# The sample's matmul runs are placed behind the prompt's value products, and the gates are multiplied five blocks later

## The chip, the cores and the metric

The kernel runs on one core of one Trainium2 chip. A core has a matrix engine (TensorE, PE in the profile; its weight loads are shown apart as PEld), a vector engine (VectorE, DVE), a scalar engine (ScalarE, ACT), a general engine (GpSimd, POOL) and a queue engine (SyncE, SP) that issues most transfers here; 16 DMA engines move the data. Each engine works through its own list of instructions in order, and semaphores tie the lists together. The metric is the device time of one execution in microseconds.

## What is computed

One inference step of a small hybrid decoder, in float32, for two groups of tokens at once: a prompt of 2048 new tokens, and a sample of 8 sequences with 8 new tokens each, which look back on 4096 cached positions. One recurrent layer (RG-LRU) comes first, then keys, values and a forget term are made once from its output, then one attention layer uses them:

```python
def fox_block(q, k, v, cq, ck, q_pos, k_pos):
    s = jnp.einsum('bqhd,bkhd->bhqk', q, k).astype(jnp.float32) * (HEAD_DIM ** -0.5)
    s = s + jnp.swapaxes(cq, 1, 2)[:, :, :, None] - jnp.swapaxes(ck, 1, 2)[:, :, None, :]
    mask = k_pos[None, :] <= q_pos[:, None]
    s = jnp.where(mask[None, None], s, -jnp.inf)
    p = jax.nn.softmax(s, axis=-1)
    return jnp.einsum('bhqk,bkhd->bqhd', p.astype(v.dtype), v)
...
def fox_mixer(x, k, v, cq, ck, q_pos, k_pos, w_in, w_out):
    z = x @ w_in
    q = z[..., :D_ATTN].reshape(B, T, N_HEADS, HEAD_DIM)
    g = z[..., D_ATTN:]
    o = fox_attention(q, k, v, cq, ck, q_pos, k_pos).reshape(B, T, D_ATTN)
    return (o * jax.nn.silu(g)) @ w_out
```

There are 16 heads of width 64. The prompt attends to itself (`_p` outputs); the sample attends to `past_k = cache_k[page_table]`, 32 pages of 128 rows for each of the 8 sequences, and to its own new rows. All keys and values of the cache together are what the sample has to read: 8 x 32 pages of 512 KB each, twice.

## The kernel before

The program is written in Python, which traces instructions in an order of its own; a planner then orders each engine's list at build time, by a simulated clock: what is ready and of the highest priority (normally the earliest traced) goes first. `tc.add_manual_dep(..., ORDER)` and `tc.issue_after` force one instruction behind another on its engine, and `tc.high_priority()` lets a block go ahead of what is traced before it.

The stages are: the recurrent layer in two chunks; the shared projection of keys, values, queries and gates (`phase_b`), with the decode of the sample beside it; the prompt's attention (`attention`), with the rest of the decode beside it; and the output projection (`project`).

**The prompt's attention.** 64 units of (head, 512 queries) are worked in blocks of 128 keys; there are 640 blocks, and the loop at line 1585 counts them as `tick`. A block has two score matmuls `st` (lines 1592, 1593), on the diagonal a third (1595), the exponential on ACT (1601) into a tile `p`, and, some 18 blocks ahead, one matmul `sx` (1431) whose row maximum DVE takes (1433, 1435). After every fourth block, two blocks late, `product` emits the value products `ops` of those four blocks as one uninterrupted group (`together`, 1616) and POOL adds the `p` tiles up (1620). `later.after(n, fn)` is a list of callbacks that are due n blocks on. At the end of two heads (a pair) `total` sums on PE and sends the sums away, and five blocks after the pair's last unit `norm` (1492) takes reciprocals and sends them by two small DMAs into the tile `rr` (r in the trace). For each of the four query chunks `fetch` loads the stored gate `sg` (1521), and three blocks later `gate` (1503) has one matmul `rp` (1505) spread `rr` over the partitions and POOL and DVE multiply output and gate.

**The decode beside it.** A turn is one sequence and half of the heads (16 turns; 13 of them in `phase_b`'s second half and in the attention). It has eight loads of four pages of keys and eight of values, which share four buffers `raw`, as do two helper tiles (`spare`). Keys: DVE transposes a load in two parts (1180) into `ktr` tiles, of which there are two; after four loads `scores` emits a run of 32 small matmuls `dS` (1148) for each part, into the PSUM bank with the tag "d". Then comes the softmax (`softmax`). Values: `products` emits a run of eight small matmuls `dO` (1262) for each load, and these wait for its four DMAs. `period` interleaves the loads of three neighbouring turns; every step yields a cost (a key step QK 700, a value step two times 510, a softmax step HOP 300), and `Side.along` runs the decode in proportion to the cost of the attention's blocks. `t.dl` is a list of callbacks like `later` that counts the turn's own steps: value runs were emitted one step after their load was asked for, key runs one or two steps after the transposes. PE's position for a run comes from `behind("T", first)`: it stands behind the latest `st` matmul that had been traced (line 1592 sets `place["T"]`), and the other matmuls of the run follow it at high priority.

The transfers are issued by SP in order; a load of pages waits there until its `raw` buffer is free (1093).

Of the kernel before, what the change touches and what calls it, by code (L numbers as in the profile page):

```python
# [60 lines left out]
AFT = 14  # L61

# [25 lines left out]
def tile_hawk_fox(  # L88
# [27 lines left out]

    def paged():

        return tc.issue_after(place["S"]) if "S" in place else ExitStack()

    def together(mms, after=(), beside=False):

        first = mms[0]().ins
        for d in after:
            tc.add_manual_dep(first, d.ins.name, SYNC)
        if beside:
            behind("T", first)
        with tc.high_priority(), tc.issue_after(first):
            for mm in mms[1:]:
                mm()  # L130
# [912 lines left out]
    def decode(es, turns, nraw, nktr, ahead):  # L1043
# [31 lines left out]
        def spare():  # L1075
            if ahead:
                return pool.tile([P, 2048], F32, name="sy", tag="raw", bufs=nraw)
            return pool.tile([P, 4096], F32, name="sy", tag="ktr", bufs=nktr)[:, :2048]

        def pages(cache, b, hg, g):  # L1080

            with ExitStack() as order:

                if len(last) >= 3:
# [3 lines left out]
                    skip_runtime_bounds_check_because="the table was held between the first page and the last")[1]  # L1088
            raw = pool.tile([P, 4, 512], F32, name="raw", tag="raw", bufs=nraw)
# [40 lines left out]
        def keys(t, xs):  # L1130
# [40 lines left out]
            for x in xs:  # L1171
                g, n = divmod(x, 4)
                if n == 0:
                    t.kts = [pool.tile([P, 4, 4, 256], F32, name="ktr", tag="ktr", bufs=nktr) for _ in range(2)]
# [4 lines left out]
                for pp in range(2):  # L1179
                    behind("V", V.transpose(t.kts[pp][:, n], raw[:, :, pp * 256:(pp + 1) * 256]).ins)  # L1180
                    if n == 3:
                        dl.after(1 + pp, lambda g=g, pp=pp, kt=t.kts[pp]: scores(g, pp, kt))
# [5 lines left out]
        def softmax(t):  # L1188
# [5 lines left out]
            while dl.q:  # L1194
                dl.tick()
                yield HOP

# [52 lines left out]
        def values(t, xs):  # L1250
# [83 lines left out]
    def attention(es):  # L1334
# [157 lines left out]
        def norm(pr, sums, q0, n, oT):  # L1492
# [25 lines left out]
            def fetch(qc):  # L1518
# [64 lines left out]

        for u, (h, qc) in enumerate(units):
            for k in range(nks[u]):
# [17 lines left out]
                def product(u=u, h=h, todo=pair, acc=acc, last=(k == nks[u] - 1)):  # L1603
# [6 lines left out]
                    def mm(k, lo, p, r):  # L1610
# [5 lines left out]
                    together([partial(mm, k, lo, p, r) for k, lo, p, _ in todo for r in range(2) if lo <= (2 + r) * P],  # L1616
                             [todo[-1][3]])
# [11 lines left out]
                tick += 1  # L1629
                later.tick()  # L1630
# [230 lines left out]
    place.clear()  # L1861
    side.upto(1e12)
# [38 lines left out]
```

## Time and profile before

| | us |
|---|---|
| median of 3 runs | 3023.98 |
| lowest and highest | 3017.05, 3034.43 |
| the profiled execution | 3028.43 |
| its span, first to last instruction | 3026.4 |

| engine | busy us | share of the span |
|---|---|---|
| PE | 2803.4 | 93% |
| DVE | 1805.5 | 60% |
| ACT | 1269.9 | 42% |
| POOL | 1084.4 | 36% |

The attention's first score matmul starts at 1749 us, the decode's last value run at 2709 us, the attention's last product at 2871 us; after it only the output projection is left. In the profile's rows a group is one line, engine and operation with its tiles (output <- inputs) and shapes: 128*32 in front of a shape means that the matmul uses 32 columns of the 128 x 128 array, 128*64 that it uses 64, 128*128 all. A float32 matmul of the small kind leaves two records, so a value run of 8 matmuls shows as x16, a key run of 32 as x64, a product of four blocks as x16 (x14 on the diagonal). A matmul's printed time holds its way through the array and overlaps the next; the time that it takes from the engine is read from start to start. "PEclk" is the granted clock of PE as a share of the full one.

### The profile page before, as it was taken

What the parts mean: (1) busy time and instruction counts of PE and PEld (TensorE: products, weight loads), DVE (VectorE), ACT (ScalarE), POOL (GpSimd) and SP (SyncE); (2) the same over time, 40 slices, a digit from 0 to 9 for tenths busy, and PEclk for the clock granted to TensorE, in tenths of its full rate; (3) what the DMA queues carried; (4) which work ended last, traced back from release to release, by engine and by line L of the source; (5) the groups of instructions that cost most, each with busy time, mean ns of one, the idle gap of its engine ahead of it and who ended that gap; (6) DMA issues with size and microseconds to landing.
All of it is one profiled execution on the core that took longest, in us unless ns stands there. A gap on an engine that the chain in (4) does not pass through costs nothing.

```text
span 3026.4 us, 60467 instructions
## 1 busy us (share of the span) xinstructions
PE 2803.4 (93%) x21614; PEld 2252.1 (74%) x21614; DVE 1805.5 (60%) x4012; ACT 1269.9 (42%) x2874; POOL 1084.4 (36%) x1199
## 2 busy tenths in 40 slices
PE   6998999998997999999999699998998999999998
PEld 5997789988887997888889556665665666565687
DVE  6877455425427775676564466656776756655344
ACT  4665342222125665534333234444544444355321
POOL 1653201000002653100000245665575656659422
PEclk9999999999998999999999889999999999999999
DMA  4224546888863226699999968898899888874343
GB/s 123 79 88 133 171 126 191 256 263 281 278 216 91 89 88 194 209 313 338 332 346 326 279 209 243 248 282 255 250 291 287 267 251 265 260 247 122 98 145 110
DMA packets 479103, 653.79 MB, mean 216 GB/s; under 512 B 91291, under 2 KB 277020, under 8 KB 471525
## 3 DMA queue, kind: packets, MB, share of 16 engines
q1 hardware_dynamic: 475174, 644.26, 67.4%
q10 hardware_dynamic: 3340, 3.56, 0.4%
q8 instruction: 171, 2.80, 0.4%
q0 software_dynamic: 288, 2.10, 0.2%
q14 instruction: 130, 1.06, 0.1%
HBM read 514.22 MB, written 135.16 MB: 215 GB/s over the span
## 4 chain that ended last, share of the span: by engine, by line
PE 59%; DMA 16%; DVE 9%; ACT 6%; SPq 5%; issue 3%; POOL 1%; ACTq 0%; DVEq 0%; POOLq 0%
PE ops L1612 7%; PE st L1592 4%; PE y L383 4%; PE y L384 4%; PE y L385 4%; DMA raw<-in_cache_k_dram 4%; PE sx L1431 4%; PE dO L1262 3%; DMA raw<-in_cache_v_dram 3%; PE st L1593 3%; PE dS L1148 3%; PE kv L383 3%; PE kv L385 3%; PE kv L384 3%; SPq L1093 2%
## 5 line engine op out<-in xcount | busy, mean ns | idle before, releaser
L108 POOL TENSOR_TENSOR acc<-acc,p 128x512 f32<-128x512 f32 (+3 forms) x576 | 640.9, 1114 | 347.7 <-PE ops L1612 211.2
L1601 ACT ACTIVATE p<-st 128x512 f32<-128x512 f32 (+3 forms) x576 | 291.3, 525 | 400.1 <-PE st L1593 177.5
L1180 DVE STREAM_TRANSPOSE ktr<-raw 128x1024 f32<-128x1024 f32 x256 | 308.2, 1226 | 125.1 <-DMA raw<-in_cache_k_dram 116.5
L1433 DVE TENSOR_REDUCE mxs<-sx 128x1 f32<-128x512 f32 x384 | 255.0, 681 | 141.0 <-PE sx L1431 139.6
L383 PE MATMUL kv<-wh,xh 128*128 128x256 f32 (+3 forms) x1088 | 310.0, 288 | 6.4 <-ACT wh L427 4.7
L384 PE MATMUL kv<-wl,xh 128*128 128x256 f32 (+3 forms) x1088 | 309.3, 287 | 5.7 <-DVE wl L428 5.7
L385 PE MATMUL kv<-wh,xl 128*128 128x256 f32 (+3 forms) x1088 | 309.6, 286 | 2.7 <-DMA xl<-xld 2.7
L1592 PE MATMUL st<-qa,ka 128*128 128x512 f32 (+3 forms) x640 | 269.9, 422 | 13.3 <-ACT p L1601 7.5
L1612 PE MATMUL ops<-p,vvt 128*64 128x256 f32 (+1 forms) x2176 | 262.9, 369 | 1.0 <-ACT p L1601 0.7
L1431 PE MATMUL sx<-kbt,qbt 96*128 96x512 f32 (+3 forms) x640 | 229.2, 416 | 29.9 <-DMA qbt<-qd 24.2
L1113 POOL TENSOR_TENSOR qw<-qb,amask 128x128 f32<-128x128 f32 x64 | 29.1, 460 | 618.1 <-PE dS L1148 325.3
L428 DVE SCALAR_TENSOR_TENSOR wl<-wst,gv,wh 128x256 fp32r<-128x256 f32 (+1 forms) x384 | 169.4, 504 | 131.8 <-ACT wh L427 131.5
L427 ACT ACTIVATE wh<-wst,gv 128x256 fp32r<-128x256 f32 (+1 forms) x384 | 164.6, 499 | 190.2 <-DMA wst<-in_w_kv_dram 72.7
L1593 PE MATMUL st<-qbt,kbt 128*128 128x512 f32 (+3 forms) x640 | 236.9, 370 | 0.0
L383 PE MATMUL qg<-xh,wh 128*128 128x512 f32 (+2 forms) x640 | 229.4, 359 | 0.0
L384 PE MATMUL qg<-xl,wh 128*128 128x512 f32 (+2 forms) x640 | 228.2, 357 | 0.0
L385 PE MATMUL qg<-xh,wl 128*128 128x512 f32 (+2 forms) x640 | 227.5, 356 | 0.6 <-DVE wl L428 0.6
L1612 PEld LDWEIGHTS ops<-p,vvt 128*64 128x64 f32 x2176 | 161.5, 141 | 88.2 <-issue 19.8
L383 PEld LDWEIGHTS kv<-wh,xh 128*128 128x128 f32 (+1 forms) x1088 | 203.5, 188 | 13.2 <-ACT wh L427 6.8
L384 PEld LDWEIGHTS kv<-wl,xh 128*128 128x128 f32 (+1 forms) x1088 | 203.2, 188 | 10.1 <-DVE wl L428 6.9
L385 PEld LDWEIGHTS kv<-wh,xl 128*128 128x128 f32 (+1 forms) x1088 | 204.8, 188 | 7.0 <-issue 3.7
L1592 PEld LDWEIGHTS st<-qa,ka 128*128 128x128 f32 x640 | 123.7, 193 | 112.8 <-issue 54.4
(297 smaller groups left out, 6356.3 us busy)
## 6 DMA issues: line engine op xcount, KB each, us to landing
raw<-in_cache_k_dram SPq DMA_DIRECT2D x512, 256.0 KB
raw<-in_cache_v_dram SPq DMA_DIRECT2D x512, 256.0 KB
wst<-in_w_kv_dram SPq DMA_DIRECT2D x48, 512.0 KB
wst<-in_b_w_in_dram SPq DMA_DIRECT2D x48, 512.0 KB
xt<-in_x_prompt_dram SPq DMA_DIRECT2D x32, 512.0 KB
wst<-in_a_w_in_dram SPq DMA_DIRECT2D x64, 256.0 KB
out_dram<-kf SPq DMA_DIRECT2D x128, 128.0 KB
sc<-cd SPq DMA_DIRECT2D x16, 1024.0 KB
```

Of the source, the lines that this page charges most:

```text
L108: eng.tensor_tensor(out, a, b, op=op)
L383: T.matmul(ps, lh(k), rh(k), start=(k == 0), stop=False)
L384: T.matmul(ps, lh(k), rl(k), start=False, stop=False)
L385: T.matmul(ps, ll(k), rh(k), start=False, stop=(k == nk - 1))
L428: V.scalar_tensor_tensor(wl[:, k, :], st[:, k, :], gk, f(wh[:, k, :]), op0=ALU.mult, op1=ALU.subtract)
L1180: behind("V", V.transpose(t.kts[pp][:, n], raw[:, :, pp * 256:(pp + 1) * 256]).ins)
L1431: T.matmul(ps[:, :w], qb[0:96, j * P:(j + 1) * P], kb[0:96, ck * 512:ck * 512 + w], start=True, stop=True)
L1433: place["V"] = V.reduce_max(mx[:, j, ck:ck + 1], ps[:, :w], axis=AX.X).ins
L1592: place["T"] = T.matmul(ps[:, lo:], ka[:, ks], qa[:, lo:], start=True, stop=False).ins
L1593: T.matmul(ps[:, lo:], kb[:, ks], qb[:, lo:], start=False, stop=(k < qc * 4))
L1601: pair.append((k, lo, p, A.activation(p[:, lo:], ps[:, lo:], AF.Exp)))
L1612: return T.matmul(ops[r * HD:(r + 1) * HD, a0 * P:], vvs[h % 2][:, k, :], p[:, :].rearrange("p (a r c) -> p a r c", a=2, r=2)[:, a0:, r, : ...
```

## The change

A new class `Runs` holds the decode's key and value runs while the attention is going (`runs.open`). `add` queues a run with the block from which it is due: 2 blocks on for a value run, 4 on for a key run. After every `product`, `beside` emits the due runs at the head of the queue, the first matmul at high priority too, and `place["T"]` now is the last matmul of that product; two key runs don't go behind one product, since they share a bank. Runs that are not emitted in time are forced out: before a `raw` buffer is asked for that one of them still holds (`slot`), before the `ktr` tiles are reused, at the begin of the softmax, and before a turn's last product. Value runs 2 to 7 of a turn are queued at once when their load is asked for, runs 0 and 1 as before after one or two steps. Outside of the attention the queue is shut, and `add` emits at once.

The gates of a pair are multiplied 8 blocks after their load is asked for instead of 3 (`GATE`); the fetch of the second two is moved so that it stays behind the store of the first two: 14 + 8 + 4 instead of 14 + 7 blocks behind the first two.

```diff
+GATE = 8
...
+    class Runs:
+        def __init__(self):
+            self.q, self.open, self.near, self.slots, self.t = [], False, False, 0, 0
+        def add(self, bank, slot, fn):
+            self.q.append((bank, slot, fn, self.t + (4 if bank else 2)))
+            if not self.open:
+                self.force()
+        def force(self, n=0):
+            while len(self.q) > n:
+                self.q.pop(0)[2]()
+        def beside(self):
+            used, self.near = set(), True
+            while self.q and self.q[0][3] <= self.t and not (self.q[0][0] and self.q[0][0] in used):
+                used.add(self.q[0][0])
+                self.q.pop(0)[2]()
+            self.near = False
+        def slot(self, n):
+            self.slots += 1
+            while any(s is not None and s <= self.slots - n for _, s, _, _ in self.q):
+                self.q.pop(0)[2]()
...
     def together(mms, after=(), beside=False):
-        first = mms[0]().ins
+        with tc.high_priority() if runs.near else ExitStack():
+            first = mms[0]().ins
...
+        last = first
         with tc.high_priority(), tc.issue_after(first):
             for mm in mms[1:]:
-                mm()
+                last = mm().ins
+        return last
...
+            runs.slot(nraw)
             raw = pool.tile([P, 4, 512], F32, name="raw", tag="raw", bufs=nraw)
...
                 if n == 0:
+                    runs.force(1)
                     t.kts = [pool.tile([P, 4, 4, 256], F32, name="ktr", tag="ktr", bufs=nktr) for _ in range(2)]
...
+                    if n == 0 and pp == 1:
+                        runs.force()
                     behind("V", V.transpose(t.kts[pp][:, n], raw[:, :, pp * 256:(pp + 1) * 256]).ins)
                     if n == 3:
-                        dl.after(1 + pp, lambda g=g, pp=pp, kt=t.kts[pp]: scores(g, pp, kt))
+                        run = partial(scores, g, pp, t.kts[pp])
+                        if runs.open:
+                            runs.add("d", None, run)
+                        else:
+                            dl.after(1 + pp, run)
...
                 yield HOP
+            runs.force()
...
-                dl.after(2 if ahead and x == 0 else 1, lambda i=x * 4, raw=raw, came=came: products(i, raw, came))
+                slot = runs.slots
+                run = partial(products, x * 4, raw, came)
+                if runs.open and x > 1:
+                    runs.add(None, slot, run)
+                else:
+                    dl.after(2 if ahead and x == 0 else 1, partial(runs.add, None, slot, run))
...
-            dl.after(1, lambda: new_products(t.rown))
             dl.flush()
+            runs.force()
+            new_products(t.rown)
...
-                later.after(3, lambda: gate(qc, sg))
+                later.after(GATE if n == 4 else 3, lambda: gate(qc, sg))
...
-                later.after((3 + 2 * (qc % 2) + (AFT + 7) * (qc // 2) if n == 4 else 2 * (qc - q0)), lambda qc=qc: fetch(qc))
+                later.after((3 + 2 * (qc % 2) + (AFT + GATE + 4) * (qc // 2) if n == 4 else 2 * (qc - q0)), lambda qc=qc: fetch(qc))
...
+        runs.open = True
         for u, (h, qc) in enumerate(units):
...
-                    together([partial(mm, k, lo, p, r) for k, lo, p, _ in todo for r in range(2) if lo <= (2 + r) * P],
-                             [todo[-1][3]])
+                    place["T"] = together([partial(mm, k, lo, p, r) for k, lo, p, _ in todo for r in range(2) if lo <= (2 + r) * P],
+                                          [todo[-1][3]])
+                    runs.beside()
...
                 tick += 1
+                runs.t = tick
                 later.tick()
```

More of the change, by code (lines that the diff above doesn't have):

```diff
@@ L115, in behind @@
             tc.add_manual_dep(ins, place[engine].name, ORDER)
+    class Runs:
[18 more added lines that the diff above has]
+                self.q.pop(0)[2]()
+    runs = Runs()
     def paged():
@@ L1088, in pages @@
                     skip_runtime_bounds_check_because="the table was held between the first page and the last")[1]
+            runs.slot(nraw)
             raw = pool.tile([P, 4, 512], F32, name="raw", tag="raw", bufs=nraw)
@@ L1861, in tile_hawk_fox @@
     place.clear()
+    runs.open = False
+    runs.force()
     side.upto(1e12)
```

## The prediction

> **What bounds the kernel now.** I read the page's busy table first, then the busy times of each engine by stretch. The 640 key blocks of the prompt's attention fill the last third; until 2710 us the sample's cache pages run beside them, and only there does the change act.
>
> ```profile
> span 3026.4 us, 60467 instructions
> PE 2803.4 (93%) x21614; PEld 2252.1 (74%) x21614; DVE 1805.5 (60%) x4012; ACT 1269.9 (42%) x2874; POOL 1084.4 (36%) x1199
> ```
> ```profile
> 1800.00:2710.00 910.00, 855.72 (x7807) 546.10 (x7808) 591.78 (x1262) 413.45 (x1027) 563.10 (x537) 0.97 0.86 265
> ```
>
> Columns of the second: stretch, its length, busy PE, PEld, DVE, ACT, POOL, granted PE clock, DMA share, GB/s. From 1800 to 2710 PE is busy 855.7 of 910 us, DVE 592, POOL 563, ACT 413, the DMA engines 0.86. PE, which works in order, bounds this stage; its time is matmuls, 54 us of idleness, and a clock at 0.97 (3% of 910, 27 us, lost). So I took PE's instructions by line and shape, and who let PE wait, both from 1700 to 2710.
>
> ```profile
> L1612 PE MATMUL ops<-p,vvt 128*64 128x256 f32 x1436 | 203.0, 398 | 0.5 <-ACT p L1601 0.3
> L1262 PE MATMUL dO<-raw,sx 128*32 128x256 f32 x1312 | 89.5, 394 | 20.1 <-DMA raw<-in_cache_v_dram 19.4 <-issue 0.5
> L1148 PE MATMUL dS<-ktr,qw 128*32 128x128 f32 x2304 | 71.8, 278 | 0.5 <-DVE ktr L1180 0.5
> L1612 PE MATMUL ops<-p,vvt 128*64 128x128 f32 x432 | 58.0, 279 | 0.0
> L1612 PE MATMUL ops<-acc,vvt 128*64 128x256 f32 x216 | 36.6, 419 | 1.1 <-ACT p L1601 0.6 <-ACT acc L1601 0.2
> L1481 PE MATMUL tot<-acc,ones 128*32 128x512 f32 x104 | 14.8, 638 | 2.1 <-DVE mxs L1433 2.1
> L1163 PE MATMUL dS<-sy,qw 128*32 128x8 f32 x288 | 10.6, 177 | 0.0
> L1505 PE MATMUL rp<-r,sel 128*128 128x512 f32 x24 | 10.4, 479 | 11.3 <-DMA r<-rs 11.3
> ```
> ```profile
> PE dO L1262 <- DMA raw<-in_cache_v_dram: 19.4, 13, 3.1
> PE rp L1505 <- DMA r<-rs: 11.3, 5, 4.2
> PE st L1592 <- ACT p L1601: 5.9, 17, 0.8
> PE sx L1431 <- DVE mxs L1435: 2.8, 6, 0.7
> ```
> ```profile
> SPq L1093 <- PE dO L1262: 33.0, 12, 7.3
> ```
>
> A value run leaves 16 records, a key run 64: 1312/16 = 82 value runs and 2304/64 = 36 key runs of the sample, 10.25 turns of 8 value runs. The prompt's value products are (1436 + 432 + 216)/16 = 130 groups, one for every four blocks: 520 blocks in 1010 us, at most 1.94 us each. A turn is 22,615 of the kernel's cost units, so 10.25 x 22,615 / 520 = 446 units pass per block.
>
> **The change part by part: the order on PE.** What a run costs beyond its own matmuls stands in PE's timeline.
>
> ```profile
> 2106.64 1.07 PE L1262 MATMUL dO<-raw,sx 128*32 128x256 f32 x16 [1.86 <-DMA raw<-in_cache_v_dram]
> 2107.64 0.50 PE L1431 MATMUL sx<-kbt,qbt 96*128 96x512 f32 x1
> 2107.98 0.40 PE L1593 MATMUL st<-qbt,kbt 128*128 128x512 f32 x1
> 2108.31 1.52 PE L1612 MATMUL ops<-p,vvt 128*64 128x256 f32 x14
> 2109.76 0.50 PE L1592 MATMUL st<-qa,ka 128*128 128x512 f32 x1
> 2110.10 0.39 PE L1593 MATMUL st<-qbt,kbt 128*128 128x512 f32 x1
> 2110.33 0.54 PE L1431 MATMUL sx<-kbt,qbt 96*128 96x128 f32 x2
> ...
> 2132.72 1.07 PE L1262 MATMUL dO<-raw,sx 128*32 128x256 f32 x16
> 2133.72 1.52 PE L1612 MATMUL ops<-p,vvt 128*64 128x256 f32 x14
> 2135.17 1.96 PE L1148 MATMUL dS<-ktr,qw 128*32 128x128 f32 x64
> 2137.05 0.91 PE L1431 MATMUL sx<-kbt,qbt 96*128 96x512 f32 x3
> ```
>
> I go by starts. A full-width matmul of 512 columns that is followed by another takes 0.23 us (2110.10 to 2110.33); followed by a column-tiled one, 0.33 (2107.98 to 2108.31): +0.10 to enter. The first full-width one after a tiled group takes 0.34 (2109.76 to 2110.10; 2107.64 to 2107.98): +0.10 after leaving. One excursion among full-width matmuls so costs about 0.195 us beside its work. Where groups adjoin, nothing more is paid: 1.45 us for the 14-record product between full-width matmuls (2108.31 to 2109.76) and also between a value run and a key run (2133.72 to 2135.17), 1.00 for the value run both times. So a run placed behind a product saves one excursion, 0.195 us.
>
> Here the Trainium skill, in "TensorEngine Tiling (Array Packing)", section Key Properties, speaks against the change: "Mode switching requires drain", and 128x64 to 128x32 is a switch of mode too. By that rule a merged pair still pays its middle boundary, the saving is one boundary of four, half of mine, and the sum below would be 5 us smaller; the adjoining groups show no such extra, so the measurement decides.
>
> How many merge? A run is due 2 (value) or 4 (key) blocks after it is queued and then waits for a product, one in four blocks. By the code, per turn, these are forced out earlier instead: value run 0 (its buffer is asked for again two loads later), runs 5 and 7 (forced 1020 units, 2.3 blocks, after being queued), the second key run of the later half with value run 4 stuck behind it (forced after about 6 blocks, when due only at 4 and when the first key run has used that product's bank), and most of the two key runs of the earlier half. With neighbours I count 3.7 forced excursions a turn, 38 in all. Now there are 130 + 82 + 36 groups, 13 sums (104/8) and 9 runs for new keys (288/32), 270 in all; 24 of them follow another tiled group directly (two do in the rows above), which leaves 246 excursions. 130 + 13 + 9 + 38 = 190 remain. **56 x 0.195 = -11 us.** Bounds: 0 (nothing merges) and -18 (nothing forced, 152 remain).
>
> **The gates.** rp waits for the small load of r, 11.3 us in 5 cases, longest 4.2. Five blocks are 9.7 us, so all of it goes. What stands behind it:
>
> ```profile
> 2070.87 0.70 PE L1505 MATMUL rp<-r,sel 128*128 128x512 f32 x2 [2.91 <-DMA r<-rs]
> 2344.69 1.01 PE L1505 MATMUL rp<-r,sel 128*128 128x512 f32 x2 [4.18 <-DMA r<-rs]
> 2481.61 1.19 PE L1505 MATMUL rp<-r,sel 128*128 128x512 f32 x2 [2.88 <-DMA r<-rs]
> 2618.09 1.94 PE L1262 MATMUL dO<-raw,sx 128*32 128x256 f32 x16 [3.15 <-DMA raw<-in_cache_v_dram]
> ```
> ```profile
> 2071.80:2075.20 3.40, 3.40 (x16) 1.64 (x16) 1.54 (x3) 0.00 (x0) 2.54 (x2) 0.50 0.94 358
> 2344.90:2348.30 3.40, 3.40 (x11) 2.39 (x11) 1.89 (x3) 0.84 (x2) 1.25 (x1) 0.50 0.62 217
> 2481.40:2488.20 6.80, 6.59 (x26) 4.83 (x26) 2.58 (x4) 1.26 (x3) 3.04 (x4) 0.50 0.98 352
> 2618.00:2624.80 6.80, 6.71 (x35) 2.99 (x35) 2.42 (x3) 0.00 (x0) 2.38 (x2) 0.50 1.02 315
> ```
>
> Right behind each long idle time PE's granted clock is 0.50 for 3.4 or 6.8 us. The three behind rp sum to 13.6 us at half speed, 6.8 us lost. **Gates: -11.3 - 6.8 = -18 us.** Ends: -18, and 0 if another wait takes the place. The Trainium skill, "TensorE: Matmul & The Clock Gate", section HAM oscillation, asks for no idle gap over about 3.4 us; by that only the 4.18 would have cost clock, and the gates would bring 13 us, the sum 5 less. The rows show 2.91 and 2.88 followed by 0.50 as well, so I keep 18. Behind the later gate hang the oT buffers (five; the fourth unit of the next pair asks for one at about the block at which the third gate now frees it): a wait of ACT's copy of a block at most, hidden by the second half of the ops bank. The sg fetches and stores move with the gates and are off the path.
>
> **The page buffers.** A value run now comes 2 + 1.5 blocks after queueing on average instead of 510 units (1.1 blocks): 2.4 blocks, 4.6 us, later. Its raw buffer, one of four, comes free later by that, and so do the DMA issues on SP behind it (33 us in 12 cases already wait for a value run), and with them SP's q, key and gate loads. But the next value run is later by as much, so the time a page has to land stays about the same, more where a key's buffer is reused, less for keys behind a value run. Today's price is 19.4 us of waits plus half clock behind some of them (3.4 us lost after the 3.15 alone; some 7 in all). Ends: -26 (all gone) to +53 (below); I take -5, near zero since both ends of the loop move together.
>
> **What is late next.** The scores now come denser between products: PE waits on ACT's exp 5.9 us and on DVE's maxima 2.8; I take +5 for both, ends 0 and +15. Transposes of the fifth key page wait for key runs forced just before: +2, ends 0 and +5 (DVE has 318 us free in the stretch). The shared-projection stage and everything after 2710 are emitted as before: 0, since the queue is shut there or empty.
>
> **Sum**: -11 - 18 - 5 + 5 + 2 = -27 us. The profiled execution took 3028.4 us, 4.4 above the median of 3024.0; on the median 3024 - 27 = **2997 us**, 0.9% faster. A difference of 0.5%, 15 us, is about what a measurement of this kernel tells from none.
>
> **The rivals.**
> Pages become the bound (slower). The chain of waits shows the loop, where one run's buffer takes the next value page:
>
> ```profile
> 2117.49 1.10 PE dO L1262 x16
> 2118.61 0.33 SPq L1093
> ...
> 2120.20 5.63 DMA raw<-in_cache_v_dram
> ...
> 2126.07 1.07 PE dO L1262 x16
> ```
>
> Place: value runs 1 to 4 of a turn. From run to run this loop takes 8.6 us, and two successive products are 7.8 us apart, so such a link waits 0.8 us at least, more on busier DMA engines. If each of three links a turn, 31 in all, waits 2 us (62) and a third of the waits draw a half-clock window of 3.4 us (17 lost), that is 79 against today's 26: +53, with -29 from order and gates and +7 for the denser scores +31: 3055 us. It decides once such waits pass 26 + 29 - 7 = 48 us. For it: 13 of 82 runs wait already. Against it: both ends of each link move.
>
> The order's gain comes back (no change). If ACT, DVE or the DMA share of 0.86 set the pace once PE is quicker, the 11 us turn into waits and only the gates remain, less the +7: 3024 - 18 + 7 = 3013 us. For it: DMA has 14% free at most. Against it: PE is 94% busy.
>
> The runs don't land behind the products. Instructions are ordered at build time by readiness; if pages look late there, runs slip among the scores again: gates alone, 3024 - 18 = 3006 us, with half the order's saving 3000; this belongs to the forecast's side.
>
> **How the numbers follow.** Forecast with its neighbours (2968 to 3008): 0.60. No change: 0.20. Pages bound: 0.20. The range must hold eight in ten: from 2968, where every page wait also goes and nothing new waits (-11 - 18 - 26 = -55, 2969), to 3040, the middle of the slower cases (0.5% slower is 3039). The likeliest case alone: 2975 to 3008.
>
> **What would show it.** Right: rows of dO and dS stand directly behind ops in PE's timeline, excursions near 190 between 1700 and 2710, no idle time before rp, a granted clock above 0.97 in the stretch. Wrong: idle before dO above 40 us, SP's wait for dO grown well over 33 us, ACT or DVE waits before st and sx above 20 us, or new half-clock stretches.

## The result, and the profile after

The changed kernel takes 3055.04 us (median of 7 runs, 3045.79 to 3062.62), the kernel before on the same chip 3028.65 us (median of 7, 3017.05 to 3036.67): a ratio of 1.0078, 95% interval 1.0051 to 1.0104. It is slower, where 0.9% faster was forecast.

The page of the changed kernel's profiled execution, and the busy times (PE, PEld, DVE, ACT, POOL, granted PE clock, DMA share, GB/s) of the stretch that was shown of before:

```profile
span 3053.3 us, 60441 instructions
PE 2809.5 (92%) x21614; PEld 2258.5 (74%) x21614; DVE 1800.2 (59%) x4012; ACT 1268.7 (42%) x2874; POOL 1080.3 (35%) x1199
```
```profile
1800.00:2710.00 910.00, 840.41 (x7637) 537.65 (x7633) 577.00 (x1235) 402.46 (x1004) 549.21 (x526) 0.95 0.85 257
```

PE does the same 21,614 matmuls. In the stretch of 910 us it gets through 7,637 instead of 7,807 of them, is idle for 70 us instead of 54, and its clock is 0.95 instead of 0.97. Outside of the attention nothing was lost: its first score starts at 1746.4 us (1749.2 before), and 202.5 us follow the start of its last one in both kernels. From the first to the last score the attention takes 1104 us instead of 1075; these 29.7 us, less the 2.8 by which it starts earlier, are the whole difference of 26.9 us between the two profiled executions.

Who let PE wait, from 1740 to 2725 us (us in total, times, longest), and below it SP's wait for a value run:

```profile
PE sx L1480 <- DVE mxs L1482: 19.8, 13, 4.8
PE sx L1480 <- DVE mxs L1484: 12.0, 10, 3.5
PE dO L1305 <- DMA raw<-in_cache_v_dram: 11.4, 7, 2.8
PE st L1642 <- ACT p L1651: 8.9, 24, 1.4
PE ops L1662 <- ACT p L1651: 6.4, 13, 2.4
PE rp L1554 <- DMA r<-rs: 4.1, 2, 2.5
PE dS L1198 <- DVE sc L109: 3.9, 2, 2.0
```
```profile
SPq L1128 <- PE dO L1305: 22.9, 8, 6.8
```

The two waits that the change was meant to meet did shrink: value runs wait 11.4 us for their pages (19.4 before), the gates 4.1 us for r (11.3). SP waits less for value runs too (22.9 us, 33.0 before). In their place stands a wait that hardly existed: the `sx` matmuls wait 32 us for DVE to take an earlier maximum out of their PSUM bank.

Why DVE is late is in its own waits, after (three rows) and before (two rows):

```profile
DVE ktr L1218 <- DMA raw<-in_cache_k_dram: 48.9, 17, 6.7
DVE sums L1544 <- DMA sums<-cs: 24.0, 6, 6.8
DVE sy L1193 <- DMA rawn<-ksd: 15.7, 5, 6.1
```
```profile
DVE sums L1495 <- DMA sums<-cs: 10.2, 5, 3.5
DVE ktr L1180 <- DMA raw<-in_cache_k_dram: 7.1, 4, 4.0
```

The transposes of the sample's keys wait for their page 48.9 us instead of 7.1. DVE works in order, so the maxima of the prompt stand behind a transpose that waits. One such chain, in DVE's timeline, PE's timeline, and the busy times of the 6.8 us behind it:

```profile
2388.62 2.37 DVE L1218 STREAM_TRANSPOSE ktr<-raw 128x1024 f32<-128x1024 f32 x2 [5.89 <-DMA raw<-in_cache_k_dram]
2390.91 1.25 DVE L1482 TENSOR_REDUCE mxs<-sx 128x1 f32<-128x512 f32 x2
```
```profile
2386.59 0.28 PE L1480 MATMUL sx<-kbt,qbt 96*128 96x256 f32 x1
2391.62 0.80 PE L1480 MATMUL sx<-kbt,qbt 96*128 96x512 f32 x1 [4.75 <-DVE mxs L1482]
2392.22 0.63 PE L1642 MATMUL st<-qa,ka 128*128 128x512 f32 x1
2392.64 0.63 PE L1643 MATMUL st<-qbt,kbt 128*128 128x512 f32 x1
```
```profile
2388.30:2395.10 6.80, 3.48 (x10) 2.24 (x11) 6.41 (x11) 0.92 (x2) 5.79 (x5) 0.50 1.01 349
```

DVE stands still for 5.89 us for a key page, then has two transposes to do (2.37 us) before the maximum; PE, which reached the next `sx` at 2386.9, gets its bank at 2391.6; and from 2388.3 on its clock is 0.50 for 6.8 us, so that the scores behind start 0.42 us apart instead of 0.23. Of the 11 `sx` waits above 0.7 us, 7 follow a DVE wait of 2 to 7 us for a key page, and three more a DVE wait for another load (the prompt's sums twice, the sample's new key rows once).

From the trace's PE rows between the first and the last score I took three sums: idle time, time at the half clock, and the number of excursions into column-tiled groups. Idle time went from 63.0 to 83.9 us. Half-clock time went from 70.1 to 102.6 us; half of it is lost, but only where PE works in it, and that part went from 66.9 to 90.9 us. So +20.9 us of idleness and +12.0 us of clock make 32.9 us, 3.2 more than the 29.7 by which the attention is longer. These 3.2 us are all that fewer excursions can have brought; they went from 280 to 231, which at 0.195 us each would be 9.6.

### The profile page after: what moved, and what is told of

The parts are those of the page before. It is cut to its first block, busy times and chain, and to the rows that moved or that the text cites. A ratio compares the mean times of both kernels' runs of the same rounds, so it can differ in the third digit from the quotient of the medians.

```text
span 3053.3 us, 60441 instructions
## 1 busy us (share of the span) xinstructions
PE 2809.5 (92%) x21614; PEld 2258.5 (74%) x21614; DVE 1800.2 (59%) x4012; ACT 1268.7 (42%) x2874; POOL 1080.3 (35%) x1199
## 4 chain that ended last, share of the span: by engine, by line
PE 55%; DMA 19%; DVE 10%; ACT 6%; SPq 5%; issue 4%; POOL 1%; ACTq 0%; DVEq 0%; POOLq 0%
PE ops L1662 7%; DMA raw<-in_cache_k_dram 5%; PE y L416 4%; PE y L418 4%; PE y L417 4%; PE st L1642 4%; PE sx L1480 3%; PE st L1643 3%; PE dO L1305 3%; PE kv L416 3%; PE kv L418 2%; PE kv L417 2%; PE dS L1183 2%; SPq L1128 2%; DMA raw<-in_cache_v_dram 2%
## 5 line engine op out<-in xcount | busy, mean ns | idle before, releaser
L1480 PEld LDWEIGHTS sx<-kbt,qbt 96*128 96x128 f32 x640 | 118.4, 201 | 114.3 <-issue 42.6
```

The lines of the kernel that those rows point to most:

```text
L1480: T.matmul(ps[:, :w], qb[0:96, j * P:(j + 1) * P], kb[0:96, ck * 512:ck * 512 + w], start=True, stop=True)
```

## The experiments

Times are given as the ratio to the kernel before, run beside it on the same chip, with the 95% interval. The last five columns are counted in each kernel's trace between the attention's first and last score: the length, PE's idle time, its time at half clock, the waits of `sx` for DVE (us), and the excursions.

| kernel | ratio | attention | idle | half clock | sx for DVE | excursions |
|---|---|---|---|---|---|---|
| before | 1 | 1075 | 63.0 | 70.1 | 4 | 280 |
| changed | 1.0078 (1.0051 to 1.0104) | 1104 | 83.9 | 102.6 | 32 | 231 |
| gates | 1.0043 (1.0017 to 1.0069) | 1090 | 76.2 | 79.1 | 4 | 278 |
| runs | 1.0054 (1.0030 to 1.0078) | 1091 | 81.3 | 72.2 | 15 | 237 |
| keys_only | 1.0083 (1.0051 to 1.0115) | 1095 | 78.1 | 78.8 | 14 | 272 |
| values_only | 1.0106 (1.0063 to 1.0149) | 1117 | 102.9 | 93.9 | 26 | 236 |
| due_now | 1.0056 (1.0038 to 1.0075) | 1090 | 74.8 | 81.6 | 14 | 233 |
| apart | 1.0032 (1.0011 to 1.0052) | 1083 | 66.9 | 74.6 | 13 | 291 |
| apart_old | 1.0039 (1.0016 to 1.0062) | 1086 | 70.2 | 71.7 | 11 | 279 |
| before_halfk | 1.0029 (1.0009 to 1.0049) | 1093 | 76.0 | 88.7 | 7 | 281 |
| after_halfk | 1.0023 (1.0000 to 1.0045) | 1092 | 76.4 | 94.1 | 26 | 234 |
| before_act | 1.0052 (1.0028 to 1.0076) | 1093 | 81.9 | 84.3 | 8 | 282 |
| after_act | 1.0127 (1.0093 to 1.0161) | 1124 | 97.7 | 122.2 | 20 | 229 |
| due_old_act | 1.0173 (1.0140 to 1.0206) | 1125 | 95.9 | 128.2 | 14 | 246 |
| before_fetch | 1.0039 (1.0019 to 1.0059) | 1087 | 74.7 | 76.9 | 5 | 283 |
| before_hop | 1.0046 (1.0022 to 1.0070) | 1084 | 67.0 | 78.9 | 7 | 283 |
| before_late | 1.0067 (1.0046 to 1.0089) | 1099 | 78.6 | 104.2 | 6 | 278 |
| after_late | 1.0018 (0.9995 to 1.0040) | 1072 | 69.4 | 55.3 | 10 | 232 |
| after_hop | 1.0049 (1.0032 to 1.0065) | 1091 | 73.9 | 85.0 | 24 | 232 |
| after_late_hop | 1.0039 (1.0022 to 1.0055) | 1093 | 70.9 | 90.4 | 14 | 240 |

A trace is of one execution, and one kernel's executions differ by some 10 us either way, so the ratios decide and the columns say where to look. In the ranges below, 0.1% is 3 us.

**Which half of the queue.** The changed kernel with the value runs emitted as before (keys_only), or with the key runs emitted as before (values_only).

```diff
 keys_only
-                if runs.open and x > 1:
-                    runs.add(None, slot, run)
-                else:
-                    dl.after(2 if ahead and x == 0 else 1, partial(runs.add, None, slot, run))
+                dl.after(2 if ahead and x == 0 else 1, run)
 values_only
-                        if runs.open:
-                            runs.add("d", None, run)
-                        else:
-                            dl.after(1 + pp, run)
+                        dl.after(1 + pp, run)
```

> The changed kernel, but value runs are emitted as before the change; only key runs go behind the products, and the gates stay late. Buffer theory (a value run that comes later holds its raw buffer longer, so key pages land late, DVE waits for them, and PE waits for DVE's maxima): the raw buffers are held as before, DVE's waits for key pages fall from 49 us back under 20 and PE's waits of sx for DVE from 32 under 10; the time is 10 to 25 us below before. Density rival (the scores between two products come too close together for DVE and ACT, whatever the buffers do): a third of the runs is still moved, PE's waits of sx stay near half of 32, and the time is between 5 us below and 10 us above before.

> The changed kernel, but key runs are emitted as before the change; only value runs go behind the products, and the gates stay late. Buffer theory: the whole loss stays, 15 to 35 us above before, DVE waits 40 us or more for key pages. Density rival: two thirds of the runs are moved, so some 10 to 20 us above before, and DVE's wait for key pages is a by-product that may fall under 30.

Measured 1.0083 and 1.0106, 25 and 32 us above before: either half alone costs as much as both together. For keys_only neither range holds, for values_only that of the buffer theory does. Their PE and DVE waits, of keys_only first:

```profile
PE dO L1305 <- DMA raw<-in_cache_v_dram: 27.5, 10, 5.0
DVE ktr L1218 <- DMA raw<-in_cache_k_dram: 27.1, 12, 7.7
```
```profile
PE sx L1477 <- DVE mxs L1481: 19.6, 10, 6.7
DVE ktr L1218 <- DMA raw<-in_cache_k_dram: 56.8, 16, 8.1
```

With only the key runs moved, value pages come later than before (27.5 us of waits, 19.4 before) and key pages too (27.1 us, 7.1 before); with only the value runs moved, the key pages alone come late (56.8 us), and `sx` pays. That the value runs' delay is the larger cause of the keys' lateness is not shown by this, though. In the traces the time from a key load's issue to its use (median over the turns, mean over a turn's eight loads) is 17.3 us before and 9.1 us in the changed kernel. It is 15.9 to 20.6 us in all seven kernels without the queue, and 9.1 to 12.6 us in all thirteen with it, keys_only (11.4) and values_only (10.9) alike. So the queue, even half of it, brings the loads of keys closer to their use in every plan tried; by which step was not found.

**Position against delay.** apart keeps the delay and the grid of four blocks, but emits the runs two blocks away from the products and not at high priority; due_now makes a value run due at once, so that it waits for the next product only.

```diff
 apart
-                    runs.beside()
...
+                if k % 4 == 3:
+                    runs.beside()
 due_now
-            self.q.append((bank, slot, fn, self.t + (4 if bank else 2)))
+            self.q.append((bank, slot, fn, self.t + (4 if bank else 0)))
```

> The changed kernel with the same due times and the same grid of four blocks, but the due runs are emitted two blocks away from the value products and without high priority: the same delay, no adjoining. Buffer theory: the loss stays and the saved excursions (about 10 us) are lost too: 25 to 45 us above before, DVE waits 40 us or more for key pages. Density rival: the runs spread the scores again, PE's waits of sx for DVE fall under 10 us and the time is between 18 us below and 5 us above before.

> The changed kernel with value runs due at once instead of two blocks later (key runs still four): they stand behind the next product, on average 1.5 blocks after queueing instead of 3.5, where before the change it was 1.1. Buffer theory: raw buffers come free two blocks (3.7 us) sooner, DVE's waits for key pages fall from 49 to 25 us or less, and the time is 0 to 25 us below before. Density rival: the runs stand behind the products just the same, so the time stays within 8 us of the changed kernel's, 20 to 35 us above before.

Apart from the products the runs make 291 excursions, as many as before, and the kernel is nevertheless at 1.0032, below the changed kernel's 1.0078; the shorter delay gives 1.0056. DVE's waits for key pages are long in both (46.4 and 42.2 us). Neither theory's range of time holds for either kernel: they lie 10 and 17 us above before. So being next to a product brought nothing that shows in the time, and two blocks less of delay did not bring the key pages in time, as the buffer theory had it (25 us of waits or less).

**The two edits one by one.** gates has only the later gates, runs only the queue; apart_old is apart with the old gates.

```diff
 gates (against before)
+GATE = 8
...
-                later.after(3, lambda: gate(qc, sg))
+                later.after(GATE if n == 4 else 3, lambda: gate(qc, sg))
...
-                later.after((3 + 2 * (qc % 2) + (AFT + 7) * (qc // 2) if n == 4 else 2 * (qc - q0)), lambda qc=qc: fetch(qc))
+                later.after((3 + 2 * (qc % 2) + (AFT + GATE + 4) * (qc // 2) if n == 4 else 2 * (qc - q0)), lambda qc=qc: fetch(qc))
```

> The kernel before with the late gates alone. If the gates are harmless (the first rp matmul of a pair stood where r was expected to have landed in both kernels, so five blocks change little there): within 9 us of before. If they are the loss that all variants so far share: 10 to 25 us above before. The prediction's step would be 13 to 18 us below.

> The changed kernel with the old gates (three blocks after their load), so the queue of runs alone. If the gates are harmless: 18 to 32 us above before, PE's waits of sx for DVE 20 us or more. If the gates are the shared loss: between 5 us below and 8 us above before.

> The queue of runs with its due times, emitted two blocks away from the products, and the old gates: the delay alone. If the later release of the raw buffers is the loss of the queue: 8 to 20 us above before, DVE's waits for key pages 35 us or more. If the place behind the products is the loss (the late gates alone cost 0.4%, the same delay with late gates 0.3%): within 8 us of before, whatever DVE waits.

1.0043, 1.0054 and 1.0039: each edit alone makes the kernel slower. gates, 13 us above before, lies in the range of a loss that all share; runs, 16 us above, in neither of its ranges; apart_old, 12 us above with 34.0 us of DVE's waits for key pages, near that of the delay. The waits of gates:

```profile
PE dO L1263 <- DMA raw<-in_cache_v_dram: 28.4, 8, 7.2
PE rp L1506 <- DMA r<-rs: 7.6, 4, 2.7
```

The gates still wait 7.6 us for r. The blocks at which the first `rp` of a pair stands in PE's order point to the reason: 103, 181, 259, 339, 422, 499 before, and 103, 186, 261, 341, 423, 501 with gates. As I read it, the planner had put the first gate of a pair to where it expected r, in both kernels; five blocks in the source moved it by 0 to 5 blocks. Meanwhile the value pages' wait rose to 28.4 us.

**Less traffic.** While the attention runs, a load of key pages brings half of each row and both transposes read that half, so the keys of half of the heads are left out; in before and in the changed kernel.

```diff
-                page = cache[ds(regs[i], 1), :, hg * 8:(hg + 1) * 8, :]
-                d = S.dma_start(raw[:, i, :], page.rearrange("o k h d -> (o k) (h d)"))
+                w = 4 if "T" in place and cache is cache_k else 8
+                page = cache[ds(regs[i], 1), :, hg * 8:hg * 8 + w, :]
+                d = S.dma_start(raw[:, i, :w * 64], page.rearrange("o k h d -> (o k) (h d)"))
...
+                half = "T" in place
...
-                    behind("V", V.transpose(t.kts[pp][:, n], raw[:, :, pp * 256:(pp + 1) * 256]).ins)
+                    behind("V", V.transpose(t.kts[pp][:, n], raw[:, :, :256] if half else raw[:, :, pp * 256:(pp + 1) * 256]).ins)
```

> The kernel before; while the attention runs, a key load brings only half of each page row (128 KB instead of 256 KB per page), and both transposes read that half, so the keys of half of the heads are left out and the compute stays in size. Control for the next run. Page theory: DMA share falls from 0.86 to about 0.70, PE's waits of dO for pages from 19 under 8 us, the time is 10 to 30 us below before. Density rival: 5 to 15 us below before.

> The changed kernel with the same half key loads. Page theory (late key pages make DVE late, and PE waits for DVE): DVE's waits for key pages fall under 15 us, PE's waits of sx for DVE under 12, and the kernel is 0 to 12 us faster than its control with half key loads, by the saved excursions. Density rival: the waits of sx stay near 20 us or more and it stays 15 to 30 us slower than its control.

1.0029 and 1.0023: with lighter key loads the changed kernel is level with its control (DVE's waits for key pages 23.6 and 21.4 us). That would fit the late key pages as its loss, but `sx` still waits 26 us in it, and DVE more than the 15 us that the page theory allowed. But the control, with a quarter of the pages' bytes taken away and nothing added, is itself 0.29% slower than before, which neither theory had foreseen.

**The head loads on ACT.** The loads of the prompt's keys and values of each head are issued by ACT instead of SP, where the transfer behind them mostly takes 5 to 9 us to issue (a stall).

```diff
-                queue[0].dma_start(f(ka[:, lo:hi]), kd_d[h * HD:(h + 1) * HD, :, lo:hi].rearrange("d x t -> (d x) t"))
-            queue[0].dma_start(vvs[h % 2][:, :, :], v_d[:, hr].rearrange("(k p) d -> p k d", p=P))
+                A.dma_start(f(ka[:, lo:hi]), kd_d[h * HD:(h + 1) * HD, :, lo:hi].rearrange("d x t -> (d x) t"))
+            A.dma_start(vvs[h % 2][:, :, :], v_d[:, hr].rearrange("(k p) d -> p k d", p=P))
```

> The kernel before; the loads of each head's keys ka and values vvt are issued by ACT instead of SP. In every trace so far the SP issue right behind the vvt load takes 5 to 9 us, 14 times while the decode runs, and the page loads stand behind it. If this stall makes the pages late: SP has no issue over 3 us there any more, PE's waits of dO for pages fall from 19 under 8 us, the time is 10 to 30 us below before. If the DMA engines set when pages land: within 8 us of before.

> The changed kernel with the same two loads on ACT. If the stall behind vvt makes pages late and through DVE costs the changed kernel its time: DVE's waits for key pages fall from 49 under 25 us, PE's waits of sx for DVE from 32 under 12, and it stands 0 to 12 us below its control with the loads on ACT. If the place behind the products costs by itself: still 10 to 25 us above that control.

> Value runs due at once, old gates, head loads on ACT: the parts together that should hurt least. If excursions are saved without late buffers or gates: 5 to 12 us below the control with the loads on ACT. If the place behind the products costs by itself: 5 to 20 us above that control.

1.0052, 1.0127, 1.0173 (the last with old gates and value runs due at once). The stall is gone: while the decode runs, none of SP's issues takes over 3 us (13 do in before), and `dO` waits 8.4 us for value pages instead of 19.4. But now ACT's exponentials come late. Two waits of PE and one of ACT in before_act, of which the first is 0.9 us in the trace of before, and one case from ACT's and PE's timelines:

```profile
PE ops L1612 <- ACT p L1601: 27.4, 12, 8.6
PE dO L1262 <- DMA raw<-in_cache_v_dram: 8.4, 4, 4.8
ACT p L1601 <- DMA raw<-in_cache_v_dram: 20.4, 4, 6.7
```
```profile
2172.74 0.33 ACTq L1406 DMA_DIRECT2D ka<-kd  x1
2173.17 0.28 ACT L1601 ACTIVATE p<-st 128x128 f32<-128x128 f32 x1 [6.65 <-DMA raw<-in_cache_v_dram]
2173.50 1.12 PE L1612 MATMUL ops<-acc,vvt 128*64 128x256 f32 x4 [5.75 <-ACT p L1601]
```

It is not the stall that went along: the next issue behind the value load on ACT takes 0.3 us. ACT waits in front of the issue of the key load `ka`, by the profile for another load to land, here 6.65 us and in five more cases 2 to 9 us, and the exponential that PE needs stands right behind it. So these kernels trade one wait for another, and what the stall costs by itself stays unmeasured. Of the ranges only that of a place that costs by itself holds, for after_act, 23 us above its control; due_old_act lies 37 us above, beyond both of its ranges.

**What a new plan costs by itself.** Since every control was slower, two kernels are meant to change nothing but the planned order: before_fetch asks for each gate's load one block later, before_hop counts a softmax step at 310 units instead of 300. before_fetch is not quite neutral, since the gates are multiplied three blocks after their load is asked for and so move by one block too; before_hop moves no gate in the source.

```diff
 before_fetch
-                later.after((3 + 2 * (qc % 2) + (AFT + 7) * (qc // 2) if n == 4 else 2 * (qc - q0)), lambda qc=qc: fetch(qc))
+                later.after((4 + 2 * (qc % 2) + (AFT + 7) * (qc // 2) if n == 4 else 2 * (qc - q0)), lambda qc=qc: fetch(qc))
 before_hop
-    QK, PV, HOP = 700.0, 255.0, 300.0
+    QK, PV, HOP = 700.0, 255.0, 310.0
```

> The kernel before with every fetch of the gates one block later and nothing else: no buffer, no work and no wait is meant to change, but the order of each engine's list is planned anew. Theory A (the loss of the changed kernel has causes of its own, above all the later page loads of the keys): within 0.15% of before, 3020 to 3032 us. Rival B (the order of the kernel before is a fortunate one, and any new plan of the attention costs about 0.3 to 0.5%): 3034 to 3043 us.

> The kernel before with the cost of a softmax step at 310 units instead of 300, so that the decode runs 0.4% of a turn slower against the attention: again nothing but the planned order is meant to change. Theory A: within 0.15% of before, 3020 to 3032 us. Rival B: 3034 to 3043 us. If the two neutral kernels lie on different sides, the order alone is worth some tenths of a per cent either way.

1.0039 and 1.0046, as rival B had it. This settles one thing: two edits that are not aimed at any buffer or wait cost about as much as gates or runs alone. The waits of before_fetch, then of before_hop, stand where before has them, some longer and some shorter, and the half-clock time is 7 to 9 us longer:

```profile
PE dO L1262 <- DMA raw<-in_cache_v_dram: 21.0, 15, 3.8
PE rp L1505 <- DMA r<-rs: 12.3, 4, 4.7
PE st L1592 <- ACT p L1601: 10.4, 27, 1.1
```
```profile
PE dO L1262 <- DMA raw<-in_cache_v_dram: 19.6, 12, 4.9
PE rp L1505 <- DMA r<-rs: 6.9, 3, 3.4
PE st L1592 <- ACT p L1601: 8.6, 25, 0.8
```

**Key transposes later.** If late key pages hold up DVE, the first transpose of a load, traced one step (some 3 us) later, should take the wait away. In both kernels while the attention runs:

```diff
+                late = "V" in place
+                if late:
+                    yield QK
                 for pp in range(2):
...
-                    yield QK
+                    if pp or not late:
+                        yield QK
```

> The kernel before with the first transpose of each key load traced one step (700 units, 1.6 blocks, 3 us) later, next to the second one, while the attention runs. Theory A: before has 7 us of DVE waits for key pages, so at most a few us go: 3018 to 3030 us. Rival B (any new plan costs): 3034 to 3043 us.

> The changed kernel with the first transpose of each key load traced one step (3 us) later. Theory A (key pages that come late hold up DVE, 49 us, and through it sx, 32 us, with the half clock behind): the wait at the first transpose is 2 to 7 us, so about half of it goes, DVE's waits for key pages fall to some 20 us, sx waits to some 12, and the time by 15 to 25 us, to 3030 to 3040 us. Rival B (the order): no less than the changed kernel's 3055 less 5, 3050 to 3060 us, and sx waits move elsewhere.

The changed kernel came from 1.0078 to 1.0018, at the edge of theory A's range; before went to 1.0067, 20 us above, beyond both of its ranges. The waits of after_late:

```profile
PE sx L1484 <- DVE mxs L1486: 5.9, 9, 1.3
PE sx L1484 <- DVE mxs L1488: 2.9, 6, 1.4
DVE ktr L1221 <- DMA raw<-in_cache_k_dram: 39.1, 15, 6.6
```

`sx` waits 9 us instead of 32, though DVE's waits for key pages only fell from 49 to 39, not to the expected 20. One plan may be a fortunate one, so both changed kernels were run once more, under the neutral 310 units.

```diff
-    QK, PV, HOP = 700.0, 255.0, 300.0
+    QK, PV, HOP = 700.0, 255.0, 310.0
```

> The changed kernel with the cost of a softmax step at 310 units instead of 300, a neutral new plan of its order. Theory A (the changed kernel has a loss of its own through late key pages, DVE and sx, whatever the plan): ratio 1.005 to 1.010, sx waits for DVE of 20 us and more. Rival B (its loss was one plan's misfortune among plans that lie some 0.4% above before): ratio 1.002 to 1.006 and sx waits near the 4 to 15 us of other kernels.

> The changed kernel with the first transpose of each key load one step later, and the softmax step at 310 units: a neutral new plan of the kernel that measured 1.0018. Theory A (the later transposes are the cure): again 15 to 25 us faster than the changed kernel with the same 310 units, ratio near 1.002, sx waits for DVE near 10 us. Rival B (that plan was a fortunate one): ratio 1.005 to 1.008, no difference from the changed kernel with 310 units beyond 10 us.

1.0049 and 1.0039, medians of 3038.76 and 3040.11 us: no difference, as rival B had it, though after_hop's 24 us of `sx` waits are those of theory A. The waits of after_hop, then of after_late_hop:

```profile
PE sx L1480 <- DVE mxs L1482: 10.5, 11, 2.8
PE sx L1480 <- DVE mxs L1484: 10.1, 9, 5.0
DVE ktr L1218 <- DMA raw<-in_cache_k_dram: 29.7, 13, 5.4
```
```profile
PE sx L1484 <- DVE mxs L1486: 10.7, 13, 2.7
PE dO L1309 <- DMA sx<-pd: 4.1, 1, 4.1
DVE ktr L1221 <- DMA raw<-in_cache_k_dram: 13.0, 8, 4.1
```

The later transposes did again what they should: 13.0 us of waits for key pages instead of 29.7, 14 us of `sx` waits in the table instead of 24. But it was not worth time: other waits took the place (a value run 4.1 us for `sx<-pd`), and the half-clock time rose from 85.0 to 90.4 us. So the gain of 0.6% that after_late has over the changed kernel did not come again under a second plan. The theory that late key pages make the changed kernel slow is not borne out as an explanation of its time: DVE waits 46.4 us for them in apart, at 1.0032, and 39.1 us in after_late, at 1.0018, but only 2.2 us in before_late, at 1.0067. As a mechanism of the waits in the changed kernel's own trace it stands.

## Why the prediction was wrong

Forecast were -27 us, measured +26. Three steps of the sum failed: the gates (-18 us, +13 when made alone), the waits for what is late next (+7 us, +36 of such waits measured), and a term that is not in it, what a new plan costs by itself (0.4% in two kernels). The order on PE and the page buffers were right in sign for their own rows, but their gain does not show in the time.

**The order on PE: right in kind, the gain taken elsewhere.** The merged rows are there. One excursion with both groups, from PE's timeline:

```profile
2101.36 0.40 PE L1643 MATMUL st<-qbt,kbt 128*128 128x512 f32 x1
2101.60 0.40 PE L1480 MATMUL sx<-kbt,qbt 96*128 96x512 f32 x1
2101.93 1.52 PE L1662 MATMUL ops<-p,vvt 128*64 128x256 f32 x14
2103.38 1.07 PE L1305 MATMUL dO<-raw,sx 128*32 128x256 f32 x16
2104.39 0.50 PE L1642 MATMUL st<-qa,ka 128*128 128x512 f32 x1
2104.72 0.39 PE L1643 MATMUL st<-qbt,kbt 128*128 128x512 f32 x1
```

From 2101.60 to 2104.72 are 3.12 us. At full clock and without idle time, the same stretch around a product of 14 alone has a median of 2.11 us in both kernels (32 and 17 cases), around a value run alone 1.66 us (21 and 3), around both together 3.12 us (9). Two stretches less one is 2.11 + 1.66 - 3.12 = 0.65 us, of which 0.46 are the two full-width starts that are only moved: 0.19 us saved, where 0.195 was used. The rule of the Trainium skill weighed there ("TensorEngine Tiling (Array Packing)", Key Properties) would have given half of it; these rows bear out the larger price. The count was off at both ends: in the stretch that was counted for the prediction the traces have 254 excursions before and 202 after (to 2727 us, where the last value run now stands) instead of 246 and 190, so 52 x 0.195 = 10 us instead of 11. Over all twenty kernels not even that is seen whole. The attention's length, less idle time and less half of the half-clock time in which PE works, averages 978.7 us in the ten kernels with 272 to 291 excursions and 975.6 in the ten with 229 to 246: 3.1 us for 46 excursions, a third of what 0.195 us each would give. That PE is busy for less time was no gain, because it then waited longer.

**The gates: the step failed.** "Five blocks are 9.7 us, so all of it goes" took the source's distance for the distance on PE. The edit moved the first `rp` of a pair by 0 to 5 blocks, since the planner, as I read it, had already placed it by its own estimate of r's arrival. It left 7.6 of 11.3 us of waits when made alone, and that kernel was 0.43% slower. In the changed kernel the waits fell to 4.1 us, and the 6.8 us of half clock behind them came back elsewhere.

**The page buffers: the sign of the value runs' waits was right (-8 us for -5), the place of the cost was missed.** The sentence "less for keys behind a value run" named the loads that came late and gave them no price. The time from a load's issue to its use, in the median over the turns, went from the keys to the values: value runs 1 to 4 from 6.0, 5.2, 7.0, 7.5 us to 12.4, 7.8, 10.8, 15.1; key loads 1 to 7 from 24, 23, 17, 18, 10, 14, 12 us to 12, 8, 8, 10, 7, 7, 7, where the loads that were waited for were used 3.5 to 9 us after their issue.

**What is late next: the step that failed by most.** "+5 for both, ends 0 and +15" and "+2, ends 0 and +5" stood for the waits on ACT, on DVE and on late key transposes. Measured: `sx` for DVE from 4 to 32 us, `st` and `ops` for ACT's exponentials from 5.9 + 0.9 to 8.9 + 6.4, +36 in all where +7 was summed. That DVE had 318 us free was no cover, since it works in order and a waiting transpose holds up the maxima behind it.

**The clock was left out of the balance.** In the sum only what was to be gained counted half-clock windows; the +5 and the +2 had none. The new waits draw them too: from 1760 to 2700 us there are 18 such windows instead of 11. On the rule weighed there (the Trainium skill, "TensorE: Matmul & The Clock Gate", HAM oscillation: no gap over about 3.4 us) these traces again disagree: of the changed kernel's 18 windows, three have a gap over 3.4 us around their start (from 5 us before it to 4 us after), and the others none longer than 2.94.

**No price for a new plan.** The neutral kernels show that a new order by itself can cost 0.39 and 0.46%, half of the 0.78%. No term of the sum and no rival had that. The rival "pages become the bound" named the measured 3055 us by luck: its path was longer waits of value runs, and they wait less.

**What stays open.** Over the plans tried, before has ratios of 1, 1.0039 and 1.0046, the changed kernel 1.0078 and 1.0049. Five pairs of kernels have the same edit on both sides, and the ratios of the changed kernel differ from its partner's by +0.78% (no edit), +0.03% (310 units), -0.49% (later transposes), -0.06% (half key loads) and +0.75% (loads on ACT): +0.2% on average, with differences of either sign. So whether the change itself, apart from its plan, costs or gains anything can't be told. Why the order of before is better than its neighbours was not found; its half-clock time (70.1 us) is the smallest of all but one kernel. That it is merely the luckiest of many plans was not tried with more plans. No kernel tried beat it: after_late, at 1.0018, is not told from it.

## What to carry to other kernels

When a planner orders the instruction lists, an edit is two edits: what it means, and a new plan. Run a neutral edit first (a cost of 310 for 300) and take its spread as the smallest effect that a reason can claim; here it was 0.4%, about as much as the gates or the queue cost alone. Put a suspected cure into both kernels and under more than one plan: the later transposes brought 0.6% under one plan and nothing under the next. Where a buffer is held longer, ask which loads come later by it and what in-order engine waits for them: in the changed kernel the new waits stood on DVE and `sx`, far from the runs that were moved.

## What the runs showed of the hardware

The granted clock falls to 0.50, for 3.4 or 6.8 us, also where the longest idle gap of PE around is short: in the changed kernel 11 of 18 windows had none over 2.5 us, three none over 0.6 us. The transfer that SP issues right behind the load of a head's values (`vvt`) mostly took 5 to 9 us to issue, whatever it was: 5.8 to 8.8 us in 13 of 15 cases in before (2.1 and 4.2 in the others), 5.0 to 9.6 us in all 15 in the changed kernel. With that load on ACT, in before_act, no issue on SP took over 3 us while the decode ran, and the one behind it on ACT took 0.3 us. Key and value runs whose matmuls alternate in groups of eight cost nothing beside the plain order: a product of 16 with both took 5.43 us in the one case at full clock, and 5.44 by the three alone (2.55 + 1.66 + 2.55) less two edges of 0.66.
